# Sums of squares drawn one by one beside the projections, pair stores one unit later, and five slots each for raw weights and for pairs, in a Mamba-2 and latent-attention decoder

## The chip, the cores and the metric

The kernel runs on one core of a Trainium2 chip, as a single program. The metric is the device time of one execution in microseconds. Its instructions are placed on TensorE (PE, with weight loads as PEld), VectorE (DVE), ScalarE (ACT), GpSimd (POOL) and SyncE (SP), whose queue issues most of the DMA transfers.

## The reference, cut to what matters

There are 2048 tokens of width 1024 in fp32, two layers and a last RMS norm. The first layer is a Mamba-2 mixer, the second latent attention with 16 heads.

```python
def mamba2_mixer(h, w_in, conv_w, conv_b, dt_bias, A_log, D_skip, g_out, w_out):
    proj = h @ w_in                                   # 1024 -> z 2048, xBC 3072, dt 32
    z, xBC, dt_raw = jnp.split(proj, [D_INNER, D_INNER + CONV_DIM], axis=-1)
    xBC = jax.nn.silu(causal_depthwise_conv(xBC, conv_w, conv_b))
    xs, Bm, Cm = jnp.split(xBC, [D_INNER, D_INNER + SSM_GROUPS * SSM_STATE], axis=-1)
    ...
    y = ssd_chunked_scan(xh, dt, A, Bm, Cm)           # 32 heads in 4 groups, state 128
    y = (y + D_skip[:, None] * xh).reshape(Bsz, S, D_INNER) * jax.nn.silu(z)
    y = y.reshape(Bsz, S, SSM_GROUPS, D_INNER // SSM_GROUPS)
    y = y * lax.rsqrt(jnp.mean(y * y, axis=-1, keepdims=True) + EPS)
    return (y.reshape(Bsz, S, D_INNER) * g_out) @ w_out
...
h = h + mamba2_mixer(rms_norm(h, g_pre[0]), ...)
k_nope, k_rope, v = mla_shared_kv(h, ...)             # latent of 256, rotary key of 32
h = h + mla_mixer(rms_norm(h, g_pre[1]), k_nope, k_rope, v, ...)   # causal attention, gate, back
return rms_norm(h, g_final)
```

## The kernel before, in words

**Tiles and stages.** The Mamba layer works in 16 items: four blocks b of 512 tokens, each with four head groups g. For an item there are `xbc(b, g)`, the product with the columns of B and C (kind 0, two banks) and of x (kind 1, four banks) with convolution and silu; `zgate(b, g)`, the product with the z columns (kind 2); `ssd(b, g)`, the scan over four chunks of 128 tokens, in 20 pieces; and `outp(b, g)`, the product back to width 1024. Then come the latent projections, attention (its instructions in an order of their own) and the product back.

**Products.** Every wide product is three matmuls (L86 to L88) on pairs: a value is kept as a high and a low half, in fp16 for the projections. An fp16 pair needs its weights scaled first by a power of two, so that the low half stays in range. `scan(g, kinds, ...)` finds that power: it loads the weights of a group, squares them on ACT with a running sum (L180), adds the sums on DVE, and `powers` sums over the partitions with a small matmul (L144) and makes from it the scales `up`, `down` and `half` with some eight small DVE instructions. No pair of a group can be made before its powers.

**Weights in the first block.** In block 0, `wpair` loads two raw fp32 tiles into slots `wraw` (L206; there are `WRAW` = 3), makes the pair in a slot `wsp` (`WSP` = 6) with `pair16` (ACT, L117, then DVE, L118), and stores the pair to DRAM (`wi_d`, L209). Later blocks load it from there (L211). `outp` does the same through `wunit` (raw load L130, stores to `wo_d` L551, later loads L546), in fp32 halves. All these transfers are issued in order by the SP queue: a store whose pair is not yet made keeps what stands behind it. For group 0 the squared tiles are held and used as raws (`big`, `hs`, `yT`); for the other groups they go through four slots `hx` and are loaded again as raws.

**Order of the work.** `mamba()` walks the items. Beside `ssd` of one item stand the parts of others: `outp` of the item before, `xbc` and `zgate` of the next, and at some items a part more: `scan(g + 2)` in the first two items, `head_scale()` at b = 1, g = 0, and the next block's `prep` and `steps` at g = 2. The parts run one behind the other, and after each step of a part as many of the 20 pieces of `ssd` are issued as keep both in proportion. `head_scale` finds the scale of the attention's query and key halves in 21 pieces: a raw load (L420), a square on ACT (L421), and a few DVE instructions at its end. Code issued there is then placed by a scheduler, with loads and splits of weights raised in priority (`AHEAD`).

**Names in the trace.** `big<-cumT` (L662) is the load of the decay sums that `ssd` needs for each chunk; L674 and L676 work on it, L696 is the product with it. `steps` has its 16 products in L573. `ss` are the sums of squares, `yt` the tiles that the squares are written to.

Of the kernel before, what the change touches and what calls it, by code (L numbers as in the profile page):

```python
# [21 lines left out]
P = 128  # L22
T = 2048
D = 1024
# [5 lines left out]
TB = 512  # L30
NB = T // TB
KD = D // P
NEG = -1.0e30
WRAW = 3
WSP = 6
AHEAD = 10
UPS = (0, 1, 2, 3, 6, 4, 5)
NP = 24
# [31 lines left out]
class Net:  # L70
# [52 lines left out]
        self.raws = self.raws[::-1]  # L123
        return self.t(self.sp, self.raws[0], [P, TB], bufs=2)

    def wunit(self, src, n, scale=None, late=False):

        with self.tc.high_priority(AHEAD):
            raw = self.raw(late)
            self.nc.sync.dma_start(raw[:, :n], src)  # L130
            if late:
# [29 lines left out]
        c0 = (2 - kind) * DI + g * 512  # L161
        return w[:, c0:c0 + 512]

    def scan(self, g, kinds, place, hold=False):

        nc = self.nc
        ss = self.t(self.sm, "ss", [P, 3, 4], bufs=2)
        for kind in kinds:
            per = 4 if kind == 0 else 2
            for i in range(KD // per):  # L170
                x = place(kind)
                n = D // per
                for j in range(per):
                    d = x[:, j * n:(j + 1) * n]
                    nc.sync.dma_start(d.rearrange("p (n c) -> p n c", n=2) if kind == 0 else d,
                                      self.w_in(kind, g, per * i + j))
                    if hold:
                        self.held[kind, g, per * i + j] = d
                junk = self.t(self.sp, "yt", [P, D], BF16, bufs=2)
                nc.scalar.activation(junk, x, AF.Square, accum_out=ss[:, kind, i:i + 1])  # L180
                yield
            if kind == 0:
                nc.vector.tensor_tensor(ss[:, 0, 0:1], ss[:, 0, 0:1], ss[:, 0, 1:2], ALU.add)
            else:
                nc.vector.tensor_reduce(ss[:, kind, 0:1], ss[:, kind, :], AX.X, ALU.add)
        lo, hi = kinds[0], kinds[-1] + 1
        self.powers(ss[:, lo:hi, 0], hi - lo, self.up[:, g, lo:hi], self.down[:, g, lo:hi])
        nc.vector.tensor_scalar(self.down[:, g, lo:hi], self.down[:, g, lo:hi], self.xdown, None, ALU.mult)
        if hi == 3:
            nc.vector.tensor_scalar(self.half[:, g:g + 1], self.down[:, g, 2:3], 0.5, None, ALU.mult)  # L190
        yield

    def wpair(self, b, kind, g, k, w):

        if k in w:
            return w.pop(k)
        nc, n = self.nc, 256 if kind == 0 else 512
        with self.tc.high_priority(AHEAD):
            u = self.t(self.wp, "wsp", [P, 2, 2, n], F16, bufs=WSP)
            d = self.wi_d[kind][g, k // 2]  # L200
            if b == 0:
                for j in range(2):
                    raw = self.held.pop((kind, g, k + j), None)
                    if raw is None:
                        raw = self.t(self.wp, "wraw", [P, TB], bufs=WRAW)[:, :n]
                        nc.sync.dma_start(raw.rearrange("p (n c) -> p n c", n=2) if kind == 0 else raw,  # L206
                                          self.w_in(kind, g, k + j))
                    self.pair16(u[:, j, 0], u[:, j, 1], raw, self.up[:, g, kind:kind + 1])
                nc.sync.dma_start(d, u)  # L209
            else:  # L210
                nc.sync.dma_start(u, d)  # L211
        w[k + 1] = u[:, 1, 0], u[:, 1, 1]
        return u[:, 0, 0], u[:, 0, 1]
# [99 lines left out]
    def mamba(self, cp):  # L313
# [6 lines left out]
        self.held = {}  # L320
# [7 lines left out]
        def together(*parts):  # L328
            for group in zip_longest(*parts):
                yield  # L330

        hold = self.scan(0, (0,), lambda kind: first.pop(0), True)
# [74 lines left out]
    def head_scale(self):  # L407
# [8 lines left out]
        at = [0, 0, 0]  # L416
        for i, src, gain in pieces:
            n = src.shape[1]
            raw = self.t(self.wp, "wraw", [P, TB], bufs=WRAW)
            nc.sync.dma_start(raw[:, :n], src)  # L420
            nc.scalar.activation(self.t(self.sp, "yt", [P, D], BF16, bufs=2)[:, :n], raw[:, :n], AF.Square,  # L421
                                 scale=gain, accum_out=ss[:, i, at[i]:at[i] + 1])
            at[i] += 1
            yield
# [105 lines left out]
    def outp(self, b, g):  # L530
# [7 lines left out]
        for n in range(2):  # L538
            banks = [self.t(self.pp, "mm", [P, TB], bufs=4) for _ in range(4)]

            def weights(j):
                r0, d = g * 512 + j * P, self.wo_d[g, n, j]
                if b:
                    with self.tc.high_priority(AHEAD):
                        u = self.t(self.wp, "wsp", [P, 2, TB], F32R, bufs=WSP)
                        nc.sync.dma_start(u.bitcast(F32), d)  # L546
                    return [u[:, i, :] for i in range(2)]
                w = self.wunit(a["ssm_w_out"][r0:r0 + P, n * 512:(n + 1) * 512], 512,
                               self.go[:, 4 * g + j:4 * g + j + 1])
                for i in range(2):  # L550
                    nc.sync.dma_start(d[:, i], w[i].bitcast(F32))  # L551
                return w

            def product(bank, j, i, w, start, stop):
# [785 lines left out]
```

## Time and profile before

| | |
|---|---|
| median of three runs | 3186.62 us (3184.37 to 3187.11) |
| the profiled execution | 3185.83 us, span 3184.1 us |
| mean granted clock of TensorE | 0.993 |
| bytes moved | 454.75 MB, mean 143 GB/s |

The span runs from the first to the last instruction of the profiled execution, so about 1.7 us of that execution's time lie outside it. Windows of the trace are cut at the first x-projection product of each item. A line in the waits names an engine's instruction, what released it, and then total time, times and longest; "SPq" is SP's queue. In a timeline row stand start and duration in microseconds.

### The profile page before, as it was taken

To read this page: it belongs to the slowest core of one execution; us is meant where nothing else is said; L and a number is where in the kernel's file an instruction comes from. 1 tells how busy PE (TensorE), PEld (TensorE's weight loads), DVE (VectorE), ACT (ScalarE), POOL (GpSimd) and SP (SyncE) were. 2 spreads that over 40 slices of the span, in tenths; PEclk is the share of its full clock that TensorE was granted. 3 is DMA by queue.
4 is the path that set the end of the run, shared out by engine and by line. 5 is a ranking of instruction groups with operands and counts; after the bars stand their busy time and mean duration, and the time that the engine had idled before them with its cause. 6 is when DMAs were issued, how large, how long until landed. Compare 5 with 4: busy or idle time off the path is not lost.

```text
span 3184.1 us, 51344 instructions
## 1 busy us (share of the span) xinstructions
PE 3059.6 (96%) x17746; PEld 2046.3 (64%) x17746; DVE 2394.7 (75%) x5191; ACT 1929.9 (61%) x4859; POOL 610.5 (19%) x842
## 2 busy tenths in 40 slices
PE   6999999899999999999999999999999999999998
PEld 3455555566556666655788888866666666666677
DVE  7778885677776776776967766668888888888665
ACT  8667554554544444455646554568888888888522
POOL 0212121121222111221211211222212222222100
PEclk9999999999999999999999999999999999999999
DMA  8667645433354344433565555632222322233484
GB/s 289 227 214 229 228 146 195 156 126 127 132 180 133 120 147 153 146 133 108 173 216 185 187 163 171 189 90 51 61 54 55 66 52 65 53 73 88 104 273 157
DMA packets 196586, 454.75 MB, mean 143 GB/s; under 512 B 29107, under 2 KB 52403, under 8 KB 194885
## 3 DMA queue, kind: packets, MB, share of 16 engines
q1 hardware_dynamic: 168468, 373.58, 36.0%
q0 software_dynamic: 27856, 77.89, 9.5%
q8 instruction: 140, 2.29, 0.3%
q14 instruction: 122, 0.99, 0.1%
HBM read 340.60 MB, written 110.76 MB: 142 GB/s over the span
## 4 chain that ended last, share of the span: by engine, by line
PE 64%; DVE 13%; ACT 8%; DMA 6%; issue 6%; POOL 1%; SPq 1%; ACTq 0%; DVEq 0%; POOLq 0%
PE mm L86 13%; PE mm L87 12%; PE mm L88 12%; PE tr L1081 6%; PE tr L87 4%; PE tr L86 4%; PE tr L88 3%; PE tr L1092 3%; PE tr L1091 3%; DVE cacc L500 3%; ACT Pr L1066 2%; DMA big<-cumT 2%; DMA wraw<-in_ssm_w_in_dram 1%; DVE PTs L118 1%; DVE big L674 1%
## 5 line engine op out<-in xcount | busy, mean ns | idle before, releaser
L118 DVE SCALAR_TENSOR_TENSOR PTs<-tr,PTs 128x512 f16<-128x512 f32 (+3 forms) x640 | 373.9, 605 | 77.0 <-ACT PTs L117 69.9
L1066 ACT ACTIVATE Pr<-mm,nm 128x512 f32<-128x512 f32 (+2 forms) x631 | 394.1, 635 | 49.3 <-DVE nm L1058 44.8
L1054 DVE TENSOR_REDUCE mx<-mm 128x1 f32<-128x512 f32 (+2 forms) x631 | 372.6, 602 | 32.4 <-PE mm L88 29.6
L117 ACT ACTIVATE PTs<-tr 128x512 f16<-128x512 f32 (+3 forms) x640 | 329.3, 544 | 99.5 <-PE tr L1081 97.6
L1081 PE MATMUL tr<-pack,Pr 128*128 128x128 f32 x2176 | 317.4, 273 | 1.8 <-ACT Os L1098 1.4
L86 PE MATMUL mm<-xT,wsp 128*128 128x512 f16 (+1 forms) x800 | 304.7, 381 | 0.1
L88 PE MATMUL mm<-xT,wsp 128*128 128x512 f16 (+1 forms) x800 | 303.3, 380 | 1.3 <-DVE wsp L118 1.2
L87 PE MATMUL mm<-xT,wsp 128*128 128x512 f16 (+1 forms) x800 | 303.7, 380 | 0.0
L1081 PEld LDWEIGHTS tr<-pack,Pr 128*128 128x128 f32 x2176 | 253.2, 141 | 69.1 <-ACT Os L1098 2.2
L688 ACT ACTIVATE Xw<-tr,d_wend 128x64 f32<-128x64 f32 x512 | 183.0, 358 | 133.8 <-DVE Xd L684 132.3
L86 PE MATMUL mm<-K,xT 96*128 96x512 f16 (+2 forms) x639 | 222.8, 349 | 27.2 <-ACT Pr L1066 23.7
L500 DVE SCALAR_TENSOR_TENSOR cacc<-craw,pack,cacc 128x512 f32<-128x512 f32 x288 | 213.3, 763 | 29.6 <-ACT cacc L498 28.0
L86 PE MATMUL mm<-wsp,xT 128*128 128x512 f16 (+1 forms) x640 | 232.5, 363 | 1.8 <-ACT craw L494 1.6
L87 PE MATMUL mm<-wsp,xT 128*128 128x512 f16 (+1 forms) x640 | 231.8, 362 | 0.0
L88 PE MATMUL mm<-wsp,xT 128*128 128x512 f16 (+1 forms) x640 | 231.2, 362 | 0.0
L88 PE MATMUL mm<-K,xT 96*128 96x512 f16 (+2 forms) x639 | 222.5, 348 | 0.0
L87 PE MATMUL mm<-K,xT 96*128 96x512 f16 (+2 forms) x639 | 221.7, 347 | 0.0
L1091 PE MATMUL tr<-PTs,xT 128*128 128x512 f16 (+3 forms) x640 | 221.3, 347 | 0.1
L86 PE MATMUL mm<-wsp,yT 128*128 128x512 f32 x512 | 208.4, 410 | 11.9 <-DVE sz L524 6.3
L646 POOL TENSOR_TENSOR Xp<-Xw,Xp 128x512 fp32r<-128x512 f32 x64 | 81.8, 1278 | 717.7 <-ACT Xp L645 389.6
L1092 PE MATMUL tr<-PTs,xT 128*128 128x512 f16 (+3 forms) x640 | 219.4, 347 | 0.0
L87 PEld LDWEIGHTS <-xT 96*128 96x128 f16 (+1 forms) x1152 | 112.7, 98 | 153.7 <-issue 65.0
(431 smaller groups left out, 7341.8 us busy)
## 6 DMA issues: line engine op xcount, KB each, us to landing
wsp<-wi_d SPq DMA_DIRECT2D x96, 512.0 KB, 3.7
wsp<-wo_d SPq DMA_DIRECT2D x96, 512.0 KB, 3.4
big<-cumT SPq DMA_DIRECT2D x64, 512.0 KB, 4.9
wi_d<-wsp SPq DMA_DIRECT2D x32, 512.0 KB, 3.5
wo_d<-wsp SPq DMA_DIRECT2D x64, 256.0 KB, 2.4
hx<-in_ssm_w_in_dram SPq DMA_DIRECT2D x48, 256.0 KB, 4.5
wraw<-in_ssm_w_in_dram SPq DMA_DIRECT2D x48, 256.0 KB, 3.7
wsp<-wi_d SPq DMA_DIRECT2D x48, 256.0 KB, 2.7
```

Of the source, the lines that this page charges most:

```text
L86: mm(out, l_hi, r_hi, start=start, stop=False)
L87: mm(out, l_hi, r_lo, start=False, stop=False)
L88: mm(out, l_lo, r_hi, start=False, stop=stop)
L117: self.nc.scalar.activation(hi, src, AF.Copy, scale=scale)
L118: self.nc.vector.scalar_tensor_tensor(lo, src, scale, hi, ALU.mult, ALU.subtract)
L500: nc.vector.scalar_tensor_tensor(acc, raw[:, k:k + TB], wk[k], acc, ALU.mult, ALU.add)
L688: act(Xw[:, hc], px[:, hc], AF.Copy, scale=wend[:, h0 + h:h0 + h + 1])
L1054: v.tensor_reduce(mx[:, n:n + 1], s[:, :w], AX.X, ALU.max)
L1066: nc.scalar.activation(x[:, :w], s[:, :w], AF.Exp, bias=nm, accum_out=sm[:, n:n + 1])
L1081: nc.tensor.transpose(pt[:, j * P:(j + 1) * P], st["P"][j][kb], self.ident)
L1091: nc.tensor.matmul(st["O"][:, c], vals[h][:, kb, :], u[:, 0], start=kb == 0, stop=False)
L1092: nc.tensor.matmul(st["O"][:, c], vals[h][:, kb, :], u[:, 1], start=False, stop=kb == nk - 1)
```

## The change

It is six edits that belong together.

- `WRAW` is 5 and not 3, `WSP` is 5 and not 6.
- A made pair is not stored at once: the store is noted in `owed`, and `settle()` issues it when the loads of the next unit have been issued (`wpair`, `wunit`).
- `scan` is a generator that can load `early` tiles ahead of the square it is at.
- The scan of group 0 for kinds 1 and 2 is two scans: kind 1 before the step products as before, kind 2 beside `xbc(0, 0)`. The scan of group 1, which had stood beside `xbc(0, 0)` and then `zgate(0, 0)`, stands beside `zgate(0, 0)` alone.
- The scans of groups 2 and 3 (two tiles ahead) and `head_scale` (three raws ahead) run `beneath` `xbc` and `zgate` of the next item: one of their steps before each step of the projection.
- They no longer count in the proportion: the pieces of `ssd` in those items go at 20 to 32 steps, where it was 20 to 43 and 20 to 54.

```diff
-WRAW = 3
-WSP = 6
+WRAW = 5
+WSP = 5
...
-    def scan(self, g, kinds, place, hold=False):
+    def scan(self, g, kinds, place, hold=False, early=0):
...
+        ready = []
+        for m, (kind, i, per) in enumerate(todo):
+            while len(ready) < min(m + 1 + early, len(todo)):
+                ready.append(fetch(*todo[len(ready)]))
+            junk = self.t(self.sp, "yt", [P, D], BF16, bufs=2)
+            nc.scalar.activation(junk, ready[m], AF.Square, accum_out=ss[:, kind, i:i + 1])
...
+    def settle(self):
+
+        for d, u in self.owed:
+            self.nc.sync.dma_start(d, u)
+        self.owed = []
...
             if b == 0:
+                raws = []
                 for j in range(2):
...
+                    raws.append(raw)
+                self.settle()
+                for j, raw in enumerate(raws):
                     self.pair16(u[:, j, 0], u[:, j, 1], raw, self.up[:, g, kind:kind + 1])
-                nc.sync.dma_start(d, u)
+                self.owed.append((d, u))
             else:
+                self.settle()
                 nc.sync.dma_start(u, d)
...
+        def beneath(part, other):
+            for _ in part:
+                next(other, None)
+                yield
+
         hold = self.scan(0, (0,), lambda kind: first.pop(0), True)
-        rest = self.scan(0, (1, 2), lambda kind: first.pop(0), True)
+        rest = [self.scan(0, (kind,), lambda kind: first.pop(0), True) for kind in (1, 2)]
         ahead = self.scan(1, (0, 1, 2), later)
-        for part in (hold, self.prep(0, self.g0), rest, self.steps(0), together(self.xbc(0, 0), ahead),
+        for part in (hold, self.prep(0, self.g0), rest[0], self.steps(0), together(self.xbc(0, 0), rest[1]),
                      together(self.zgate(0, 0), ahead)):
...
-                parts += [self.xbc(*items[n + 1]), self.zgate(*items[n + 1])]
+                beside = iter(())
+                if b == 0 and g < 2:
+                    beside = self.scan(g + 2, (0, 1, 2), later, early=2)
+                elif b == 1 and g == 0:
+                    beside = self.head_scale()
+                parts += [beneath(self.xbc(*items[n + 1]), beside), beneath(self.zgate(*items[n + 1]), beside), beside]
                 total += 24
...
-            if b == 0 and g < 2:
-                parts.append(self.scan(g + 2, (0, 1, 2), later))
-                total += 11
-            if b == 1 and g == 0:
-                parts.append(self.head_scale())
-                total += 22
...
-        for i, src, gain in pieces:
+        for m, (i, src, gain) in enumerate(pieces):
+            while len(raws) < min(m + 3, len(pieces)):
+                raws.append(self.t(self.wp, "wraw", [P, TB], bufs=WRAW))
...
                 w = self.wunit(a["ssm_w_out"][r0:r0 + P, n * 512:(n + 1) * 512], 512,
-                               self.go[:, 4 * g + j:4 * g + j + 1])
-                for i in range(2):
-                    nc.sync.dma_start(d[:, i], w[i].bitcast(F32))
+                               self.go[:, 4 * g + j:4 * g + j + 1], then=self.settle)
+                self.owed += [(d[:, i], w[i].bitcast(F32)) for i in range(2)]
```

The rows below are instructions in program order on one engine, with the line, the tiles (output, then inputs) and the shape; numbers behind the names tell tiles apart.

**TensorE, where the powers of group 1 are made.** Before, the small product with `ones` stands inside the kind 1 products of group 0 (`wsp_615`):

```order
L86 MATMUL mm_574<-xT_264,wsp_615 128x512
L87 LDWEIGHTS wsp_615
L87 MATMUL mm_574<-xT_264,wsp_615 128x512
L88 LDWEIGHTS wsp_615
L88 MATMUL mm_574<-xT_264,wsp_615 128x512
L144 MATMUL tr_634<-ss_440,ones 128x3
L86 LDWEIGHTS wsp_615
L86 MATMUL mm_571<-xT_272,wsp_615 128x512
L87 LDWEIGHTS wsp_615
```

Now it stands behind the last z-gate product of group 0 (`wsp_841` on `xT_304`), and the first product of group 1 (`wsp_921`) six matmuls later:

```order
L88 LDWEIGHTS xT_304
L88 MATMUL mm_713<-wsp_841,xT_304 128x512
L146 MATMUL tr_904<-ss_732,ones 128x3
L689 MATMUL tr_956<-pack,BC_517 128x128
L690 MATMUL tr_956<-BC_535,BC_517 128x128
L705 MATMUL tr_986<-pack,xs_653 128x128
L705 MATMUL tr_986<-pack,xs_671 128x128
L705 MATMUL tr_986<-pack,xs_689 128x128
L705 MATMUL tr_986<-pack,xs_707 128x128
L86 LDWEIGHTS wsp_921
L86 MATMUL mm_919<-xT_248,wsp_921 128x512
```

The scale of group 1 is thus ready before the x projection of group 0 ends in the one order, and only at the border of the groups in the other.

**SP in the first block.** Before, a store of a pair (`wi_d<-wsp`; the raws of `wsp_1167` are `wraw_1168` and `wraw_1172`) stands one pair's raws behind its own:

```order
L209 DMA wi_d<-wsp_1110 128x2048
L206 DMA wraw_1227<-in_ssm_w_in_dram 128x512
L206 DMA wraw_1231<-in_ssm_w_in_dram 128x512
L209 DMA wi_d<-wsp_1167 128x2048
L206 DMA wraw_1289<-in_ssm_w_in_dram 128x512
L206 DMA wraw_1293<-in_ssm_w_in_dram 128x512
L209 DMA wi_d<-wsp_1226 128x2048
L206 DMA wraw_1395<-in_ssm_w_in_dram 128x512
```

Now the loads of scan(2) (`hx`) come in this stretch, and a store stands two pairs' raws behind its own (those of `wsp_1225` are `wraw_1226` and `wraw_1228`, and two pairs have been loaded since):

```order
L204 DMA wi_d<-wsp_1225 128x2048
L221 DMA wraw_1444<-in_ssm_w_in_dram 128x512
L176 DMA hx_2136<-in_ssm_w_in_dram 128x512
L176 DMA hx_2170<-in_ssm_w_in_dram 128x512
L221 DMA wraw_1446<-in_ssm_w_in_dram 128x512
L204 DMA wi_d<-wsp_1301 128x2048
L221 DMA wraw_1567<-in_ssm_w_in_dram 128x512
L221 DMA wraw_1569<-in_ssm_w_in_dram 128x512
L204 DMA wi_d<-wsp_1361 128x2048
L221 DMA wraw_1612<-in_ssm_w_in_dram 128x512
L204 DMA wi_d<-wsp_1443 128x2048
L221 DMA wraw_1614<-in_ssm_w_in_dram 128x512
```

So the store of a pair has moved behind one unit's loads more, and the squared tiles of the coming group have moved ahead of raws that they had stood behind.

**SP in the item with the head scales.** Before, the raws of `head_scale` stand in one run between two loads of decay sums (`big<-cumT`), behind loads of output pairs:

```order
L546 DMA wsp_6258<-wo_d 128x1024
L662 DMA big_6129<-cumT_4101 128x1024
L420 DMA wraw_5881<-in_mla_w_uq_dram 128x512
L420 DMA wraw_5885<-in_mla_w_uq_dram 128x512
L420 DMA wraw_5900<-in_mla_w_uq_dram 128x512
L420 DMA wraw_5904<-in_mla_w_uq_dram 128x512
L420 DMA wraw_5908<-in_mla_w_uq_dram 128x512
L420 DMA wraw_5935<-in_mla_w_uq_dram 128x512
L420 DMA wraw_5939<-in_mla_w_uq_dram 128x512
L420 DMA wraw_5943<-in_mla_w_uq_dram 128x512
L662 DMA big_6343<-cumT_4101 128x1024
L420 DMA wraw_5972<-in_mla_w_uq_dram 128x512
```

Now they stand among the loads of the input pairs (`wsp<-wi_d`):

```order
L230 DMA wsp_5559<-wi_d 128x2048
L230 DMA wsp_5641<-wi_d 128x2048
L230 DMA wsp_5703<-wi_d 128x2048
L686 DMA big_5861<-cumT_4115 128x1024
L444 DMA wraw_5551<-in_mla_w_uq_dram 128x512
L444 DMA wraw_5573<-in_mla_w_uq_dram 128x512
L444 DMA wraw_5612<-in_mla_w_uq_dram 128x512
L444 DMA wraw_5655<-in_mla_w_uq_dram 128x512
L230 DMA wsp_5746<-wi_d 128x2048
L444 DMA wraw_5671<-in_kv_w_down_dram 128x32
L230 DMA wsp_5843<-wi_d 128x2048
L444 DMA wraw_5717<-in_kv_w_down_dram 128x32
```

The run of eight raws ahead of a `big<-cumT` has gone; four stand behind one such load, and then one at a time.

On the engines the counts hardly change: TensorE and DVE have one matmul and nine DVE instructions more, from the second call of `powers` for group 0. From the second block on, TensorE's order is the same as before for all but the items named.

More of the change, by code (lines that the diff above doesn't have):

```diff
@@ L124, in raw, with wunit @@
         return self.t(self.sp, self.raws[0], [P, TB], bufs=2)
-    def wunit(self, src, n, scale=None, late=False):
+    def wunit(self, src, n, scale=None, late=False, then=None):
         with self.tc.high_priority(AHEAD):
@@ L130, in wunit @@
             self.nc.sync.dma_start(raw[:, :n], src)
+            if then:
+                then()
             if late:
@@ L162, in w_in, with fetch @@
         return w[:, c0:c0 + 512]
-    def scan(self, g, kinds, place, hold=False):
+    def scan(self, g, kinds, place, hold=False, early=0):
         nc = self.nc
         ss = self.t(self.sm, "ss", [P, 3, 4], bufs=2)
[L168 to L185, printed above, removed]
+        todo = [(kind, i, 4 if kind == 0 else 2) for kind in kinds for i in range(2 if kind == 0 else 4)]
+        def fetch(kind, i, per):
+            x, n = place(kind), D // per
+            for j in range(per):
+                d = x[:, j * n:(j + 1) * n]
+                nc.sync.dma_start(d.rearrange("p (n c) -> p n c", n=2) if kind == 0 else d,
+                                  self.w_in(kind, g, per * i + j))
+                if hold:
+                    self.held[kind, g, per * i + j] = d
+            return x
+        ready = []
[4 more added lines that the diff above has]
+            nc.scalar.activation(junk, ready[m], AF.Square, accum_out=ss[:, kind, i:i + 1])
+            if i == KD // per - 1:
+                if kind == 0:
+                    nc.vector.tensor_tensor(ss[:, 0, 0:1], ss[:, 0, 0:1], ss[:, 0, 1:2], ALU.add)
+                else:
+                    nc.vector.tensor_reduce(ss[:, kind, 0:1], ss[:, kind, :], AX.X, ALU.add)
+            yield
         lo, hi = kinds[0], kinds[-1] + 1
@@ L319, in mamba @@
         self.layer_constants(cp)
-        self.held = {}
+        self.held, self.owed = {}, []
         first = [self.t(self.sp, "big", [P, D], bufs=2) for _ in range(2)]
@@ L415, in head_scale @@
         pieces += [(1, a["kv_w_down"][k * P:(k + 1) * P, 256:288], self.gk[:, k:k + 1]) for k in range(KD)]
-        at = [0, 0, 0]
-        for i, src, gain in pieces:
-            n = src.shape[1]
-            raw = self.t(self.wp, "wraw", [P, TB], bufs=WRAW)
-            nc.sync.dma_start(raw[:, :n], src)
+        at, raws = [0, 0, 0], []
+        for m, (i, src, gain) in enumerate(pieces):
+            while len(raws) < min(m + 3, len(pieces)):
+                raws.append(self.t(self.wp, "wraw", [P, TB], bufs=WRAW))
+                ahead = pieces[len(raws) - 1][1]
+                nc.sync.dma_start(raws[-1][:, :ahead.shape[1]], ahead)
+            raw, n = raws[m], src.shape[1]
             nc.scalar.activation(self.t(self.sp, "yt", [P, D], BF16, bufs=2)[:, :n], raw[:, :n], AF.Square,
```

1 line of the change is left out of this document (added).

## The prediction

> **What bounds the kernel now.** I read the page first, then the windows cut at the first x-projection product of each item, then the waits and the chain inside the windows that are longer than the others.
>
> ```profile
> span 3184.1 us, 51344 instructions
> PE 3059.6 (96%) x17746; PEld 2046.3 (64%) x17746; DVE 2394.7 (75%) x5191; ACT 1929.9 (61%) x4859; POOL 610.5 (19%) x842
> ```
>
> TensorE is busy for 96% of the span. The most that any reordering can win is its idle time, 3184.1 - 3059.6 = 124.5 us, and whatever it loses to a lower clock. So the question is where the idle time lies. The windows (columns: stretch and length; busy time and count of PE, PEld, DVE, ACT, POOL; granted clock; DMA share; GB/s) answer it for the Mamba layer:
>
> ```profile
> 0.00:20.97 20.97, 5.19 (x24) 5.10 (x25) 9.89 (x57) 14.71 (x31) 0.64 (x7) 1.00 0.95 323
> 20.97:90.68 69.71, 60.69 (x284) 28.39 (x282) 53.57 (x135) 54.15 (x102) 5.16 (x14) 0.95 0.88 285
> 90.68:197.26 106.58, 98.43 (x574) 58.92 (x573) 85.31 (x181) 76.25 (x189) 21.93 (x24) 0.95 0.69 219
> 197.26:299.20 101.94, 94.07 (x536) 54.99 (x536) 84.39 (x176) 71.96 (x171) 17.59 (x23) 0.98 0.70 227
> 299.20:404.70 105.50, 99.00 (x589) 59.14 (x587) 89.09 (x178) 65.52 (x159) 18.60 (x22) 1.00 0.64 214
> 404.70:497.00 92.30, 89.12 (x527) 53.09 (x527) 70.08 (x143) 47.93 (x125) 17.62 (x24) 1.00 0.47 158
> 497.00:604.80 107.80, 95.11 (x543) 57.07 (x543) 67.88 (x147) 57.44 (x163) 18.53 (x25) 0.94 0.52 172
> 604.80:695.80 91.00, 90.47 (x533) 53.98 (x533) 67.49 (x141) 46.68 (x125) 19.57 (x24) 1.00 0.38 128
> 695.80:797.60 101.80, 98.79 (x592) 60.05 (x590) 72.66 (x148) 48.45 (x131) 18.72 (x24) 1.00 0.40 136
> ```
>
> An undisturbed item takes 91 us (row 604.80) and one that also prepares the next block 102 us (row 695.80), both with a full TensorE. Five stretches are worse: the start and the first three items, which read raw weights, and the item at 497.00, which holds the head scales. The last has the same number of matmuls as its neighbour (543 and 533) and takes 16.8 us more.
>
> **The startup.** Waits of TensorE before 90.68, then four instructions from the timeline (start, duration; "idle before <- releaser" in brackets):
>
> ```profile
> PE tr L144 <- DVE ss L185: 7.0, 1, 7.0
> ...
> 26.25 1.06 ACT L180 ACTIVATE yt<-yT 128x1024 bf16<-128x1024 f32 x1
> 30.54 0.16 DVE L185 TENSOR_REDUCE ss<-ss 128x1 f32<-128x4 f32 x1 [3.98 <-ACT yt L180]
> 30.84 0.56 PE L144 MATMUL tr<-ss,ones 128*128 128x2 f32 x2 [6.99 <-DVE ss L185]
> 31.34 5.17 PE L573 MATMUL tr<-xT,wdt 128*64 128x512 f16 x16
> ```
> ```profile
> 374.95 3.64 PE L573 MATMUL tr<-xT,wdt 128*64 128x512 f16 x16
> ```
>
> TensorE waits 7.0 us for the sum of eight squares. The last four, on yT, are of the z weights; they begin at 26.25 and end at 30.4. The change computes the power of kind 1 from the first four alone, so the wait ends 4.2 us sooner. The sixteen step products behind it took 5.17 us, and 3.64 us in the next block: another 1.5 us, if the shorter idle time (2.8 us) keeps the clock up. [...]
>
> The four squares do not vanish. They come after the first splits on ACT, 4.2 us in a stretch where ACT is busy 54.15 of 69.71 us, with one more powers matmul and nine small DVE instructions of 0.16 us; kind 2 is needed only after the x projection of the whole item. I give this 1 us (0 to 2). More costly is that scan(1) starts beside the z-gate and not beside the x projection: its powers matmul now stands right behind the last z-gate product, six small matmuls ahead of the first product of group 1. The pair of that product needs the powers, nine DVE instructions at 0.16 us, one ACT split and one DVE split, some 3 to 5 us with queueing, of which the six matmuls cover about 2. I take +3 (0 to +5). Startup: -4.2 - 1.5 + 1 + 3 = -1.7, about **-2**.
>
> **Items one to three.** Waits of SP between 90.68 and 299.20 (total, times, longest), and two groups of the same window:
>
> ```profile
> SPq L209 <- DVE wsp L118: 43.8, 18, 12.5
> SPq L206 <- DVE wsp L118: 25.1, 14, 3.5
> SPq L551 <- ACT wsp L112: 23.2, 10, 8.7
> ```
> ```profile
> L117 ACT ACTIVATE wsp<-wraw,up 128x512 f16<-128x512 f32 (+1 forms) x41 | 26.0, 672 | 18.6 <-DMA wraw<-in_ssm_w_in_dram 16.5 <-PE mm L88 1.1 <-PE tr L88 0.6
> L180 ACT ACTIVATE yt<-hx 128x1024 bf16<-128x1024 f32 x20 | 21.4, 1072 | 2.7 <-DVE y L703 1.8 <-DMA hx<-in_ssm_w_in_dram 0.7
> ```
>
> The SP queue stands for 43.8 us in front of stores of pairs (L209) that are not yet split and for 23.2 us in front of stores of output units (L551); loads of raw weights queue behind them. ACT in turn waits 16.5 us for raw weights. That is the loop which the change opens: a store goes out behind the next unit's loads, and five raw slots let them start earlier (L206 waits 25.1 us for a slot). The squares (20 of 1.07 us) stay, with two loads ahead, and are spread over the projections.
>
> How much reaches TensorE? In the first item it is idle 106.58 - 98.43 = 8.2 us, and a granted clock of 0.95 means 0.05 x 106.58 = 5.3 us of its work at no gain; the floor is 106.58 - 8.2 - 5.3 = 93. I take a bit over half of 13.5: **-8** (0 to -13). In the second it is idle 7.9 us, with 2.0 us in the clock; but DVE has 84.39 us of work, and in no row above is DVE busy for more than 84% (89.09 of 105.50); at 97 us it would be 87%. I take **-5** (+4 to -8). The third item has 89.09 us of DVE work and no scan; compared with 101.80 it can win 3.7 at most: **-1** (+1 to -3). The fourth is 1.3 us off the undisturbed: 0.
>
> **The head scales.** Waits in 497.00 to 604.80, three pieces of the chain (start, duration), and the squares:
>
> ```profile
> DVE big L674 <- DMA big<-cumT: 8.3, 3, 7.0
> ...
> PE tr L723 <- DVE y L718: 5.4, 1, 5.4
> ```
> ```profile
> 557.83 3.96 DMA wraw<-in_mla_w_uq_dram
> ...
> 562.66 3.69 DMA wraw<-in_mla_w_uq_dram
> ...
> 568.40 5.12 DMA big<-cumT
> ```
> ```profile
> L421 ACT ACTIVATE yt<-wraw,pack 128x512 bf16<-128x512 f32 (+1 forms) x21 | 11.8, 562 | 5.4 <-DVE y L703 3.1 <-DMA wraw<-in_mla_w_uq_dram 2.1
> ```
>
> Raw loads come in a run, three slots at a time, each slot a round of load (3.7 to 4.0 us) and square. Eight of them stand on SP between one load big<-cumT of the decay matrix and the next; DVE waits 7.0 us for that next one, and TensorE then for DVE. It loses 107.80 - 95.11 = 12.7 us of time and 0.06 x 107.80 = 6.5 us of clock. The change puts one piece beside each of the 24 projection steps, with three loads ahead: at 92 us for 32 steps, three steps are 8.6 us, over twice the landing time. The raws that stand ahead of a big<-cumT then have had their slots free for two squares. ACT needs no more than before: 57.44 of 92 is 62%. The neighbours say 91 to 92.3; the row at 497.00 says 107.8. I take 93.8, **-14** (0 to -17), nearest to the neighbours because matmuls and DVE work are theirs.
>
> **One pair slot fewer.** After the first block, loads of pairs wait for slots. Waits of SP in 800 to 1100, and of TensorE, in that order:
>
> ```profile
> SPq L211 <- PE mm L88: 122.8, 39, 6.0
> SPq L546 <- PE mm L88: 116.4, 23, 6.4
> ```
> ```profile
> PE tr L696 <- DVE big L676: 1.1, 2, 0.6
> PE tr L87 <- POOL Xp L646: 0.9, 3, 0.3
> ```
> ```profile
> wsp<-wi_d SPq DMA_DIRECT2D x96, 512.0 KB, 3.7
> wsp<-wo_d SPq DMA_DIRECT2D x96, 512.0 KB, 3.4
> ```
>
> SP waits 239 of 300 us for a slot, yet TensorE never waits for a pair. A pair of the shortest kind feeds 12 matmuls of some 0.22 us, 2.6 us; four slots ahead are 10 us against 3.7 us to land. So the fifth suffices, with 6 us to spare, and none of the twelve later items moves. In the MLA stages the splits lag by one slot, where I find no wait of TensorE now; I allow **+2** (0 to +6) for places where three units are taken together.
>
> **Sum.** -2 - 8 - 5 - 1 - 14 + 2 = -28. The profiled execution took 3185.83 us, which gives 3157.8; the median of the runs is 3186.62, 0.8 above it, so the forecast is 3158.6.
>
> **Rivals.** A: only the head scales gain. The first block stays where it is because DVE and the loads set it together: the DMA engines are 0.88 and 0.69 busy in the two rows before 197.26, and DVE 80 to 84%. For it: ACT's wait for raws is 16.5 us, but TensorE's idle time is 8 us in each item. Against it: SP's waits are for slots and order, not bytes. [...] -14 + 2 and startup -2 to +2: about 3172 (3168 to 3178).
>
> B, slower: the first block starves. Today the pairs of group 1 are split while TensorE still has group 0; after the change their powers come at the border, so no pair of the new group stands ready, and five raws are 2.5 pairs. It decides where a raw takes longer to land than two pairs feed TensorE, 2 x 2.6 = 5.2 us for the short kind. Their median landing times are
>
> ```profile
> hx<-in_ssm_w_in_dram SPq DMA_DIRECT2D x48, 256.0 KB, 4.5
> wraw<-in_ssm_w_in_dram SPq DMA_DIRECT2D x48, 256.0 KB, 3.7
> ```
>
> and 5.2 us is 16 to 41% more. Then 4 short pairs in each of three groups lose about 1.5 us each, 18 us, with the squares' loads in front of them another 10 to 15 and no gain in the block; with +5 at the border and without the full head gain the end is 3192 to 3200. Against it: by 90.68 some 27 MB have moved (20.97 x 323 + 69.71 x 285), and the rate then falls to 219 GB/s, not for want of engines (0.69): room for bursts is there.
>
> C: the first block reaches the pace of the rest, items of 93, 93 and 102: -13, -9, -3.5, with the head at -16.5 and startup -4: about 3141.
>
> D: no effect. The head loads lose their run, but big<-cumT is late again, now behind stores and loads of x, and the block gains what the border costs: 3180 to 3190.
>
> **Chances.** Forecast 0.60 (own range 3145 to 3168), A 0.17, B 0.08 (0.07 slower, 0.01 no change), C 0.07, D 0.08 (0.02 of it just faster, 0.06 no change). Two kernels of this kind can be told apart by about 0.2%, 6.4 us: 3180.2 to 3193.0 is "same". Faster is 0.60 + 0.17 + 0.07 + 0.02 = 0.86, same 0.07, slower 0.07. From 3141 to 3180 only half of C, B and most of D lie outside, under 0.2.
>
> **What would show it.** In the next profile the item with the head scales should last 92 to 96 us with a clock of 1.00, and DVE's wait for big<-cumT (8.3 us in three) should be gone; the wait of 7.0 us at the first step powers should be near 2.8; SP's wait in front of pair stores should fall from 43.8 us to a few; the first two items should end at about 98 and 97. The prediction is wrong if ACT or TensorE waits for raws more than now, if a powers matmul after the first z-gate leaves TensorE idle over 5 us, or if any item after 604.80 is longer than its row here.

## The result, and the profile after

The changed kernel took 3162.59 us, the median of six runs (3159.67 to 3165.44), against 3185.75 us for the kernel before, measured beside it: a ratio of 0.9926, 95% interval 0.9913 to 0.9939. It is 23 us faster, where 27 to 28 were forecast. The profiled execution took 3161.85 us.

The head of the page, and the windows cut at the first x-projection product of each item, with the same columns as in the prediction:

```profile
span 3160.0 us, 51410 instructions
PE 3054.2 (97%) x17748; PEld 2046.3 (65%) x17748; DVE 2393.8 (76%) x5200; ACT 1926.8 (61%) x4859; POOL 608.8 (19%) x842
```
```profile
21.27:92.42 71.15, 61.55 (x293) 29.39 (x292) 50.86 (x138) 56.83 (x106) 5.89 (x14) 0.96 0.84 284
...
92.42:192.98 100.56, 95.27 (x571) 55.90 (x572) 84.75 (x180) 76.06 (x192) 19.34 (x24) 0.98 0.72 236
192.98:290.90 97.92, 92.26 (x531) 54.56 (x531) 86.40 (x189) 70.75 (x170) 16.73 (x22) 0.98 0.73 241
290.90:397.60 106.70, 100.40 (x589) 60.65 (x586) 86.90 (x172) 62.52 (x154) 18.31 (x22) 0.98 0.61 203
397.60:488.20 90.60, 90.05 (x534) 54.08 (x534) 72.98 (x151) 53.28 (x137) 19.78 (x25) 1.00 0.51 170
488.20:578.50 90.30, 89.84 (x536) 54.28 (x536) 64.88 (x138) 52.27 (x152) 19.66 (x24) 1.00 0.59 196
```

The rest of the span, in two stretches, before and after (the items from the second of block 1 up to the last x projection, and everything behind that one's start):

```profile
604.80:1444.30 839.50, 827.89 (x4899) 498.82 (x4899) 605.98 (x1241) 414.26 (x1113) 175.75 (x216) 1.00 0.41 140
1444.30:3184.10 1739.80, 1690.14 (x9783) 1230.77 (x9780) 1328.47 (x2940) 1127.65 (x2808) 334.64 (x489) 1.00 0.42 120
```
```profile
578.50:1416.50 838.00, 827.77 (x4899) 498.75 (x4899) 608.73 (x1241) 413.74 (x1113) 174.03 (x216) 1.00 0.42 140
1416.50:3160.00 1743.50, 1691.74 (x9783) 1233.52 (x9781) 1328.26 (x2940) 1126.50 (x2808) 334.44 (x489) 1.00 0.42 120
```

Differences of these rows give the account of the 24.1 us between the two spans:

| stretch | before | after | difference | forecast |
|---|---|---|---|---|
| up to the first x product of the second item | 90.68 | 92.42 | +1.7 | -2 |
| first loop item | 106.58 | 100.56 | -6.0 | -8 |
| second | 101.94 | 97.92 | -4.0 | -5 |
| third | 105.50 | 106.70 | +1.2 | -1 |
| fourth | 92.30 | 90.60 | -1.7 | 0 |
| item of the head scales | 107.80 | 90.30 | -17.5 | -14 |
| the next items | 839.50 | 838.00 | -1.5 | 0 |
| from the last x projection on | 1739.80 | 1743.50 | +3.7 | +2 |

The largest term is the item of the head scales: it now lasts as long as an undisturbed one, with a clock of 1.00. Three terms are losses: the start, the third item and the end. The one in the third item is told with the clock in the last section. To see the first, the waits of TensorE from 14 to 100 us, and instructions at the end of the first z-gate (start, duration, idle time before and what ended it):

```profile
PE mm L86 <- ACT wsp L117: 6.0, 1, 6.0
...
PE tr L146 <- DVE ss L192: 2.8, 1, 2.8
```
```profile
85.22 0.28 PE L146 MATMUL tr<-ss,ones 128*128 128x3 f32 x2
...
87.51 0.48 DVE L698 TENSOR_SCALAR big<-big,d_cum 128x128 f32<-128x128 f32 x2 [4.56 <-DMA big<-cumT]
...
89.89 0.15 DVE L148 TENSOR_SCALAR pwx<-tr 128x3 f32<-128x3 f32 x1
...
91.62 0.16 DVE L154 TENSOR_SCALAR up<-pw 128x3 int32<-128x3 int32 x1
...
91.82 0.91 ACT L117 ACTIVATE wsp<-wraw,up 128x256 f16<-128x256 f32 x2 [0.22 <-DVE up L154]
...
92.38 0.61 PE L86 MATMUL mm<-xT,wsp 128*128 128x512 f16 x1 [6.05 <-ACT wsp L117]
```

TensorE makes the sum for the powers of group 1 at 85.22. DVE reads it only at 89.89. DVE had been idle for 4.56 us by 87.51, since the next instruction in its order was the decay work of the first chunk (L698), which waited for big<-cumT. Six of these and two z-gate instructions (L549) stood ahead of the powers, and two more decay and one more z-gate instruction came between them. `up` is written at 91.62, the split follows at once, and TensorE has waited 6.05 us. The first wait, 2.8 us for the squares of kind 1, is what the prediction had.

For the loss at the end, the waits of TensorE from 1480 to 1700, where the Mamba layer ends:

```profile
PE tr L720 <- issue: 4.1, 1, 4.1
PE tr L88 <- DVE st L113: 2.2, 2, 2.0
PE mm L86 <- DVE hs L583: 2.1, 1, 2.1
PE mm L86 <- DMA wsp<-wo_d: 1.9, 2, 0.9
```

### The profile page after: what moved, and what is told of

Its sections match the earlier page's. It is cut to its first block, busy times and chain, and to the rows that moved or that the text cites. A ratio compares the mean times of both kernels' runs of the same rounds, so it can differ in the third digit from the quotient of the medians.

```text
span 3160.0 us, 51410 instructions
## 1 busy us (share of the span) xinstructions
PE 3054.2 (97%) x17748; PEld 2046.3 (65%) x17748; DVE 2393.8 (76%) x5200; ACT 1926.8 (61%) x4859; POOL 608.8 (19%) x842
## 4 chain that ended last, share of the span: by engine, by line
PE 66%; DVE 9%; ACT 6%; issue 6%; DMA 2%; POOL 1%; SPq 0%; ACTq 0%; POOLq 0%; DVEq 0%
PE mm L86 13%; PE mm L87 13%; PE mm L88 13%; PE tr L1105 6%; PE tr L87 4%; PE tr L86 4%; PE tr L88 4%; PE tr L1116 3%; PE tr L1115 3%; DVE cacc L525 2%; ACT Pr L1090 2%; PE tr L720 1%; DVE PTs L118 1%; DMA big<-cumT 1%; ACT Xw L712 1%
## 5 line engine op out<-in xcount | busy, mean ns | idle before, releaser
L670 POOL TENSOR_TENSOR Xp<-Xw,Xp 128x512 fp32r<-128x512 f32 x64 | 82.8, 1294 | 720.3 <-ACT Xp L669 386.3
```

## The experiments

Twelve kernels ran, four to a group, each group beside the kernel before (medians of 3186.81, 3183.32 and 3181.94 us). The groups differ by that much, so between them ratios are compared. Trace figures are those of the one profiled execution.

**The head scales alone.** The kernel before, with only this edit, the `beneath` that it needs and the loop in `head_scale` that keeps three loads out (the one at hand counted):

```diff
-                parts += [self.xbc(*items[n + 1]), self.zgate(*items[n + 1])]
+                beside = self.head_scale() if b == 1 and g == 0 else iter(())
+                parts += [beneath(self.xbc(*items[n + 1]), beside), beneath(self.zgate(*items[n + 1]), beside), beside]
...
-                parts.append(self.head_scale())
-                total += 22
```

> The kernel before, with three raw slots and six pair slots, and only the head scales changed: one square beside each projection step of the item, three raws ahead. If the run of raw loads ahead of big<-cumT was the loss (theory), the item falls from 107.8 to 91 to 94 us and the time to 3168 to 3173 us. If the five raw slots were what helped (rival), three slots fill at once, big<-cumT still waits, and at least half of the gain is missing: 3178 us or more.

3170.12 us, ratio 0.9946 (0.9933 to 0.9960). The item:

```profile
497.80:589.50 91.70, 90.05 (x536) 54.28 (x535) 63.04 (x138) 52.35 (x152) 18.66 (x24) 1.00 0.56 191
```

107.80 us became 91.70 with three raw slots. So the run of squares and loads in its old place was the loss. This one edit moves the time by 16.7 us; the whole change moved it by 23.2. It does three things at once: the loads leave the run on SP, the squares leave the run on ACT, and the pieces of `ssd` go at 20 to 32 steps and not at 20 to 54.

**The head scales put back.** The changed kernel with that part undone, the loop in `head_scale` too:

```diff
-                elif b == 1 and g == 0:
-                    beside = self.head_scale()
...
+            if b == 1 and g == 0:
+                parts.append(self.head_scale())
+                total += 22
```

> The changed kernel with only the head scales put back into one run behind the projections. Theory: the loss of the item comes back, 13 to 17 us, so 3175 to 3180 us, in spite of five raw slots. Rival (five slots heal the run as well): under 3168 us.

3173.55 us, ratio 0.9959 (0.9947 to 0.9972), 1.5 us under the expectation. The item, two stretches of 10 us in it, and two waits:

```profile
486.50:590.00 103.50, 95.38 (x542) 56.99 (x541) 67.82 (x148) 57.08 (x163) 18.88 (x25) 0.95 0.54 179
...
550.00:560.00 10.00, 8.94 (x68) 6.60 (x66) 5.83 (x16) 9.93 (x36) 0.30 (x1) 1.00 0.60 186
560.00:570.00 10.00, 3.65 (x9) 1.89 (x9) 8.99 (x21) 7.89 (x30) 2.84 (x3) 0.67 0.42 126
```
```profile
DVE big L697 <- DMA big<-cumT: 1.0, 2, 0.5
...
PE tr L86 <- ACT Xp L668: 2.5, 1, 2.5
```

With five raw slots it takes 103.50 us: the slots alone heal 4.3 of 17.5 us. The rival is refuted in its strong form. But the theory's chain is not what is left: DVE waits only 1.0 us for big<-cumT here, less than in the items that run well (2.8 us with the head scales moved alone, 3.5 with the whole change). ACT is busy for 9.93 of the 10 us from 550, with eight squares among its work, and TensorE then waits for ACT and for DVE.

**scan(1) beside the first x projection again.**

```diff
-together(self.xbc(0, 0), rest[1]),
+together(self.xbc(0, 0), rest[1], ahead),
```

> The changed kernel with scan(1) begun beside the first x projection again (with the squares of kind 2 of group 0 there too), so that the powers of group 1 are made before the border of the groups. Theory: the 6.0 us wait of TensorE for the first pair of group 1 goes, with about 1 us of low clock behind it, and the time is 3155 to 3159 us. Rival: the squares delay pairs and the convolution of the first item on ACT by as much, and the time stays at 3161 to 3165 us.

3164.26 us, ratio 0.9930 (0.9917 to 0.9942): the rival's figure. The first product of the second group comes at 90.3 us, 2.1 sooner than with the change, but the last product of the first x projection starts at 69.3 and not at 64.3, and the four items of the loop take 400.90 us for 395.78. What the earlier powers win is lost again; that more squares on ACT beside the start's products are the reason is likely and not shown.

**Powers at high priority.** The squares stay, the small instructions go ahead of the rest:

```diff
-        self.powers(ss[:, lo:hi, 0], hi - lo, self.up[:, g, lo:hi], self.down[:, g, lo:hi])
...
+        with self.tc.high_priority(200):
+            self.powers(ss[:, lo:hi, 0], hi - lo, self.up[:, g, lo:hi], self.down[:, g, lo:hi])
...
```

> The changed kernel with the powers of every group given a high priority, so that those of group 1 stand early in the z-gate of group 0 on TensorE and DVE; the squares stay where they are. Theory: the DVE instructions of the powers no longer stand behind the decay work that waits for big<-cumT; the wait of 6.0 us falls under 1 us, and the time is 3155 to 3159 us. Rival: the squares are not done earlier, so TensorE only waits at the powers instead: 3161 to 3166 us.

3156.56 us in four runs, ratio 0.9902 (0.9889 to 0.9916), the lowest median here. The waits of TensorE from 14 to 100, and the windows of the start, of the four loop items of the first block, and of the end:

```profile
PE tr L146 <- DVE ss L190: 5.6, 1, 5.6
PE tr L146 <- DVE ss L192: 4.1, 2, 2.9
```
```profile
20.90:86.90 66.00, 61.06 (x286) 28.36 (x285) 50.87 (x136) 57.65 (x110) 6.01 (x14) 0.97 0.87 283
86.90:481.10 394.20, 375.38 (x2228) 224.38 (x2227) 332.97 (x691) 262.88 (x647) 74.69 (x92) 0.99 0.67 218
1411.90:3155.70 1743.80, 1691.41 (x9783) 1233.05 (x9781) 1328.09 (x2940) 1127.71 (x2808) 334.49 (x489) 1.00 0.41 119
```

The wait of 6.0 us at the border is gone, one of 1.2 us at the powers (4.1 less 2.9) stands in its place, and the second group starts at 86.9, 5.5 us sooner than with the change. The squares stayed where they were, so the loss at the border was the place of the powers in the order. The edit moves their small matmul and their DVE instructions together. In two later kernels with the same priority the ratios are 0.9931 and 0.9922. The profiled spans of all three are 4.3 to 5.7 us under the 3160.0 of the change (3155.7, 3155.0 and 3154.3); how much of this the medians keep is open.

**Stores at once.** The changed kernel with pairs stored as soon as made:

```diff
-                self.owed.append((d, u))
+                nc.sync.dma_start(d, u)
...
-                self.owed += [(d[:, i], w[i].bitcast(F32)) for i in range(2)]
+                for i in range(2):
+                    nc.sync.dma_start(d[:, i], w[i].bitcast(F32))
```

> The changed kernel with each pair stored as soon as it is made, as before; slots, scans and head scales stay changed. Theory (the order on SP holds raw loads back): SP stands in front of stores of unmade pairs again and the first block loses 4 to 8 us of its 10 to 12: 3166 to 3171 us. Rival (five raw slots are enough cover, the store's place does not matter): 3160 to 3165 us.

3161.55 us, ratio 0.9928 (0.9916 to 0.9940), the same as the change (0.9926). The theory falls: the four loop items take

```profile
93.80:486.40 392.60, 375.49 (x2220) 224.10 (x2220) 330.67 (x690) 263.38 (x651) 76.28 (x92) 0.99 0.65 215
```

against 395.78 with later stores (488.20 - 92.42). SP stands in front of pair stores for longer again, as the theory said, in 93.8 to 290:

```profile
SPq L227 <- DVE wsp L118: 46.3, 22, 17.8
```

It costs nothing. Putting the stores behind the next loads wins nothing.

**The slots put back to three and six**, the rest of the change kept (`WRAW = 3`, `WSP = 6`):

> The changed kernel with three raw and six pair slots. Theory: the 3.7 us that the last item and the first latent stage lost come back, since they lack the sixth pair slot; the first block loses 3 to 7 us for want of raws: 3160 to 3167 us. Rival (raw slots are worth nothing here): 3157 to 3160 us.

3164.49 us, ratio 0.9942 (0.9928 to 0.9955), as the theory has it. The four loop items and the end:

```profile
90.60:491.40 400.80, 376.13 (x2220) 224.17 (x2220) 335.09 (x687) 263.37 (x647) 73.73 (x92) 0.99 0.64 211
1421.70:3161.30 1739.60, 1690.24 (x9783) 1231.50 (x9781) 1328.56 (x2940) 1126.83 (x2808) 333.62 (x489) 1.00 0.42 120
```

The items lose 5.0 us of their gain (400.80 for 395.78) and the end wins 3.9 (1739.60 for 1743.50).

**The slots alone.** The kernel before with `WRAW = 5`, `WSP = 5`:

> The kernel before with five raw and five pair slots and nothing else. Theory: 3.7 us lost at the end of the Mamba layer, 4 us won in the item of the head scales (103.5 for 107.8, as in the kernel with only that run restored), 2 to 4 us in the first block: 3182 to 3186 us. Rival (raw slots are the gain of the first block): 3173 to 3178 us.

3180.68 us, ratio 0.9991 (0.9982 to 1.0000), 1.3 us under the expected range and far from the rival.

```profile
91.20:492.30 401.10, 380.00 (x2221) 227.14 (x2219) 326.36 (x675) 261.64 (x645) 77.31 (x91) 0.98 0.63 209
492.30:595.90 103.60, 95.65 (x543) 56.95 (x543) 68.05 (x148) 56.95 (x163) 19.47 (x25) 0.95 0.53 179
1435.80:3178.40 1742.60, 1690.85 (x9783) 1233.11 (x9780) 1327.54 (x2940) 1126.42 (x2808) 334.51 (x489) 1.00 0.42 120
```

By themselves the slots win 5.2 us in the four loop items (406.32 before), 4.2 in the item of the head scales, and lose 2.8 at the end.

**Powers first, with three and six slots.**

> The changed kernel with the powers at high priority and with three raw and six pair slots. Theory: 3.7 us less at the end of the Mamba layer and 3 to 7 us more in the first block than with five and five: 3156 to 3160 us. Rival (raw slots are worth nothing once the powers come in time): 3152 to 3154 us.

3172.36 us, ratio 0.9961 (0.9949 to 0.9974): both expectations missed, by 12 us and more. The start is as good as with five and five, but the first loop item is

```profile
86.50:197.70 111.20, 97.42 (x578) 57.00 (x577) 91.19 (x188) 76.27 (x189) 20.73 (x24) 0.97 0.72 234
```

111.20 us long. The waits of SP for raw slots in this item, with three slots and then with five:

```profile
SPq L222 <- DVE wsp L118: 36.8, 7, 18.3
```
```profile
SPq L222 <- DVE wsp L118: 7.2, 2, 3.8
```

With three, ACT also waits 18.1 us for raws (10.7 and 7.4 for the two kinds). So raw slots are worth little in the changed kernel (5 us in the four items) and much once the powers go first. Why that order needs them so badly I have not settled.

**Three and six slots, and stores at once.**

> The changed kernel with three raw and six pair slots and every pair stored as soon as it is made, so that scans, head scales and the first group's squares are all that is left of the change. Theory (the store's place is worth nothing, with three raw slots as with five): 3161 to 3166 us, as with three and six slots and later stores (3164.5). Rival (with three slots the stores hold the loads back): 3168 to 3174 us.

3161.99 us, ratio 0.9937 (0.9925 to 0.9950). With three slots too, later stores win nothing (0.9942). In both pairs of single traces the four items are even 3.2 us shorter with stores at once (397.60 here, 489.60 - 92.00, for 400.80), which the medians don't confirm.

**Five and five, powers first, stores at once.**

> Five and five slots, powers at high priority, every pair stored at once. Theory (the store's place is worth nothing): 3154 to 3159 us, as with later stores (3156.6). Rival (with the powers early the stores are in the way): 3160 us or more.

3159.96 us, between the two expectations; ratio 0.9931 (0.9919 to 0.9944) against 0.9902. The profiled spans of the two agree, 3155.0 and 3155.7 us, and the medians do not; whether later stores help a little here stays open.

**The value weights' products on DVE**, with powers first:

```diff
-                nc.gpsimd.tensor_tensor(raw[k], raw[k], f.bitcast(F32), ALU.mult)
+                v.tensor_tensor(raw[k], raw[k], f.bitcast(F32), ALU.mult)
```

> Five and five slots, powers at high priority, and the four products of the value weights in the last item on DVE and not on GpSimd. Theory (DVE instructions beside GpSimd's products are stretched by 1 us there and TensorE waits 4.1 us behind them): that wait shrinks to under 2 us, time 3153 to 3156 us. Rival (DVE is short in the item anyway): 3156 to 3160 us.

3157.21 us, ratio 0.9922 (0.9909 to 0.9936): not faster, as the rival has it. The wait in front of L721, 4.2 us with powers first alone, became 2.9, and the stretch from the last x projection on 1742.80 for 1743.80. So these four products are a small part of that loss at most.

**The start put back.** The changed kernel with the scans of groups 0 and 1 as before:

```diff
-        rest = [self.scan(0, (kind,), lambda kind: first.pop(0), True) for kind in (1, 2)]
+        rest = self.scan(0, (1, 2), lambda kind: first.pop(0), True)
...
-rest[0], self.steps(0), together(self.xbc(0, 0), rest[1]),
+rest, self.steps(0), together(self.xbc(0, 0), ahead),
```

> The changed kernel with the scans of groups 0 and 1 as they were before (kinds 1 and 2 of group 0 in one, scan(1) beside the first x projection). Theory: the start loses the 5 us won up to the end of the first z-gate and wins the 6 to 7 us lost at the border of the groups, so 3159 to 3163 us. Rival (the early squares keep pairs of group 1 ready and fill the ring): 3153 to 3157 us.

3165.28 us, ratio 0.9948 (0.9936 to 0.9961), above the expected range. By its trace the first product of the second group starts at 92.5 us, as with the change (92.4), and the span is 3161.2 us for 3160.0. The four items of the loop:

```profile
92.50:489.30 396.80, 375.20 (x2227) 223.55 (x2226) 334.40 (x688) 262.36 (x648) 74.37 (x92) 1.00 0.64 212
```

The edits of the start are about a wash in the trace and perhaps 0.2% by the medians; the intervals overlap.

## Why the prediction was right, and where not

**The head scales** (-14 forecast, -17.5 in the trace, 16.7 measured alone): the place of the loss was right, and the size was the end that the neighbours named, not the cautious value. The chain was right only in part. It ran from "Eight of them stand on SP between one load big<-cumT of the decay matrix and the next" over DVE's wait of 7.0 us to TensorE. With the run in its old place and five slots, that wait is 1.0 us in all and the item still takes 103.50 us, 13.2 more than with the change, so most of the loss does not hang on it. "ACT needs no more than before: 57.44 of 92 is 62%" is an average over the item; inside it ACT is full for 10 us. Which of the loads, the squares and the slower pieces of `ssd` costs how much, no run separates. The sign "DVE's wait for big<-cumT (8.3 us in three) should be gone" did not come either: it is 3.5 us in three, and TensorE waits 0.2 us behind it.

**The startup** (-2, measured +1.7): the mis-sized term. Its first half came: the wait is 2.8 us, and the first z-gate's last product comes at 85.0, 5.2 us sooner than the 90.2 of before. The 1.5 us of the clock did not. That 2.8 us of idle time would keep it up was an estimate; the clock fell behind a wait of 2.84 us too, to 0.50 from 28.15 to 31.57.

```profile
26.91 0.35 PE L146 MATMUL tr<-ss,ones 128*128 128x1 f32 x2 [2.84 <-DVE ss L192]
27.20 5.33 PE L597 MATMUL tr<-xT,wdt 128*64 128x512 f16 x16
```

The sixteen step products took 5.33 us, no less than 5.17. The border of the groups was priced at +3 (0 to +5) and cost 6.0 of waiting, with a clock of 0.50 in the 3.6 us behind it:

```profile
92.40:96.00 3.60, 3.60 (x9) 1.31 (x10) 3.03 (x9) 3.60 (x17) 0.00 (x0) 0.50 0.42 128
```

The step that failed was "nine DVE instructions at 0.16 us ... some 3 to 5 us with queueing": the price counted the chain, not what stood ahead of it on DVE: decay instructions that waited for a DMA, and z-gate work. The prediction had named the pattern ("if a powers matmul after the first z-gate leaves TensorE idle over 5 us") as what would make it wrong, and it did occur.

**Items one to four** (-14 forecast, -10.5 measured): the size was near, and one of the reasons given, the place of the stores, was wrong. "SP's wait in front of pair stores should fall from 43.8 us to a few" failed. SP waits from 92.42 to 290.90, stores of both kinds now being L204:

```profile
SPq L204 <- ACT wsp L112: 27.9, 9, 13.4
SPq L204 <- DVE wsp L118: 26.8, 21, 4.6
...
SPq L204 <- DVE wsp L113: 12.0, 11, 2.8
```

For pair stores that is 26.8 us and not a few, and 66.7 us for both kinds, against 73.1 before (the 67.0 shown in the prediction and 6.1 of L551 behind DVE); ACT still waits 14.6 us for raws. Storing at once cost nothing with five slots or with three, so that order was not the loss. What the runs show in its place are two parts of about equal size: five raw and five pair slots (5.2 us alone) and the scans in their new places (5.5 us with three and six slots, 406.32 to 400.80). Their sum is 10.7, and the change gives 10.5, each figure from one execution. Of the second part only 1.0 us goes when the scans of groups 0 and 1 are put back (396.80 for 395.78), so most of it should be those of groups 2 and 3, which no run puts back alone.

**One pair slot fewer** (+2, measured +3.7): the sign was right, the size was taken too small, and the place was right only in part. The five profiled kernels with three and six slots spend 1739.0 to 1740.2 us from the start of the last x projection on, the nine with five and five 1741.7 to 1744.9, so it is the slots; raw and pair slots were always changed together. The prediction looked for it in the MLA stages and held that none of the twelve later items moves. But the longest wait, 4.1 us in front of L720 (1.1 with three and six slots), ends at 1501.3 us, in the last Mamba item. Of the other waits, 1.9 us are for loads of output pairs (wsp<-wo_d), which a slot less may delay. For the 4.1 us the cause is not settled.

**The rivals.** A (only the head scales gain) was wrong by the 10.5 us of the first block, though most of the gain of the whole is the head's; B's mechanism at the border occurred, without starving the pairs behind it: ACT's wait for raws fell from 16.5 to 14.6 us. C's pace was not reached (100.56 and 97.92 us for 93), and of D's late big<-cumT what is left harms nothing. Nor were A's loads shown at a limit in the first rows, of 323 and 285 GB/s: from 18.00 to 24.10 us the changed kernel moves 385 GB/s. The sum of the forecast, -28, was 4 us too good by the trace: +3.7 from the start, +3.5 from the items and +1.7 from the end, less 3.5 from the head scales and 1.5 from later items. That the total came so near owes something to luck: terms 8.9 us too good stand against terms 5.0 us too cautious.

## What to carry to other kernels

When a side task of loads and squares runs in one piece beside a scan, change its place before the number of its slots: here 16 of 17.5 us against 4. A mean load of an engine (62%) says nothing of the 10 us in which the task fills it. A wait of a queue (SP's 67 us in front of stores) is no loss until something on the critical path is shown to wait for what stands behind it; later stores brought nothing here. When a small chain becomes urgent, price it from what stands ahead of it in each engine's order, above all instructions that wait for a DMA; a priority for some ten tiny instructions took a wait of 6.0 us away and 4.3 us from the profiled span.

## What the runs showed of the hardware that was not expected

The clock fell behind a wait of TensorE of 2.84 us and behind one of 1.97, and stayed up behind 3.04 us of idle time in the kernel before. In the traces of the kernel before and of the changed one, half clock lasts 3.41, 6.83 or 13.65 us, but for the very end (7.94 and 7.33), and starts in each trace at whole multiples of 3.41 us from one another, so the time may be divided into stretches of that length, from one change of the clock on. Two such stretches after, each with the one behind it, and two before:

```profile
24.74:28.15 3.41, 1.24 (x7) 0.83 (x8) 2.06 (x7) 3.41 (x10) 0.00 (x0) 1.00 0.47 115
28.15:31.57 3.42, 3.42 (x10) 1.43 (x9) 3.42 (x15) 2.55 (x6) 0.00 (x0) 0.50 0.66 240
...
359.25:362.66 3.41, 1.44 (x12) 1.13 (x10) 3.27 (x11) 3.02 (x6) 0.00 (x0) 1.00 0.20 77
362.66:366.07 3.41, 3.41 (x15) 2.95 (x15) 2.79 (x6) 2.06 (x3) 0.00 (x0) 0.50 0.00 0
```
```profile
365.55:368.97 3.42, 2.18 (x16) 1.72 (x14) 3.34 (x8) 2.92 (x7) 0.00 (x0) 1.00 0.71 226
368.97:372.38 3.41, 1.61 (x12) 1.46 (x13) 3.34 (x9) 3.19 (x6) 0.00 (x0) 1.00 0.75 240
```

Where TensorE is busy for 1.24 or 1.44 us of the 3.41, the next stretch runs at half clock; where the 3.04 us of idle time fall into two stretches and leave 2.18 and 1.61 us, it does not. Divided in this way, the two traces hold 1822 stretches at full clock that another one follows, from their first clock records (20.81 and 21.33 us) on. All 13 with under 1.40 us of busy time are followed by half clock, and none of the 1798 with over 2.00 us is; of the 11 between, three are (1.44, 1.50 and 1.92 us). So in these two traces the clock goes with the busy time in such a stretch and not with the length of a wait alone. The third item shows it: its wait of 3.04 us became 1.97, but the clock fell, and TensorE is busy there for 1.4 us more (100.40 for 99.00).

In the changed kernel a small DVE instruction, L698, is now and then stretched by about 1 us while a GpSimd product, L670, is running. One place, DVE and then POOL:

```profile
103.73 1.30 DVE L698 TENSOR_SCALAR big<-big,d_cum 128x128 f32<-128x128 f32 x1
```
```profile
103.17 1.77 POOL L670 TENSOR_TENSOR Sp<-st,Sp 128x512 fp32r<-128x512 f32 x1 [4.53 <-ACT Sp L669]
```

23 of 512 of these L698 instructions took 1.29 to 1.34 us for a median of 0.28, and every one of the 23 ended 0.08 to 0.09 us behind an L670 of GpSimd. In the place above the DVE instruction ends at 105.03 and the GpSimd one at 104.94. Why it takes so long, no run shows. Taking the four products of the value weights off GpSimd won nothing; what the stretches beside L670 cost was not tried.
